# A new place in SBUF for the operands of a two-layer encoder's matrix products

## The chip, the cores and the metric

The kernel runs on one core of a Trainium2 chip. The metric is the device time of one execution in microseconds (us). The profile and the trace come from one profiled execution of the same program. Engines are named as in the profile: PE is TensorE (PEld its weight loads), DVE is VectorE, ACT is ScalarE, POOL is GpSimd, SP is SyncE, which here only issues DMAs (SPq).

## What is computed

A trunk of two layers over 512 tokens of width 1024, in float32. Each layer: RMSNorm; one input projection whose columns are shared by four token mixers (A: dense attention with 8 query and 2 key heads; B: a gated linear recurrence in both directions behind a short convolution; C: attention in a band, with sinks; D: dilated attention in three groups) and by a sigmoid gate per mixer; each mixer's output is projected to 1024, gated and summed; an output projection; the residual. Then RMSNorm and an MLP of width 4096. After the layers comes a last RMSNorm.

```python
for l in range(DEPTH):
    hn = rmsnorm(x, norm_mix_g[l])
    proj = hn @ w_in[l]
    (aq, ak, av, bx, by, cq, ck, cv, dq, dk, dv, gl) = jnp.split(proj, split_points, axis=-1)
    ya, yb, yc, yd = ...                     # the four mixers
    gates = jax.nn.sigmoid(...)              # of gl
    merged = (gates[:, :, 0] * (ya @ w_proj_a[l]) + gates[:, :, 1] * (yb @ w_proj_b[l])
              + gates[:, :, 2] * (yc @ w_proj_c[l]) + gates[:, :, 3] * (yd @ w_proj_d[l]))
    x = x + merged @ w_out[l]
    hn = rmsnorm(x, norm_mlp_g[l])
    x = x + jnp.square(jax.nn.relu(hn @ w_mlp1[l])) @ w_mlp2[l]
return rmsnorm(x, norm_final_g)
```

## The kernel before

All tokens stay in SBUF with the features on the partitions: a tile [128, 8, 512] holds 128 x 8 features of 512 tokens, 16 KiB in each partition. Every matrix product is made of split operands. A float32 number is parted into a high part, which PE's fp32r form holds, and a low part, the rest; a product is the sum of three, high weights on high input, high on low, and low on high (`mm3`, lines 175 to 183; `several`, lines 193 to 195, does the same for some groups side by side). One matmul of this kind has weights of 128x128 (the stationary operand, loaded into the array by an instruction of its own) and a moving operand of 128 x 512, and adds into one PSUM tile. A group is 8 steps of depth, 24 matmuls.

The weights come as a stream of chunks, in an order written out ahead: `raw` (a DMA on SP's queue, line 102), `whi` (a cast on ACT, line 118), `wlo` (a subtraction on DVE, line 127). Each of the three has three buffers of 4 KiB.

The moving operands are these. `xh` and `xl`, the two parts of the normed input (without its tokens' factors), stay in one place for the whole kernel; they are written by `xg_tile` (line 237) and read by the projections, by the gates and by the first half of the MLP (`m1`). `yA` to `yD` are the mixers' outputs, read by `fill`, which works through one mixer's gates and projection: for each output tile a group on x, then four steps of depth on y. `mh` and `ml` are the parts of the merged sum, read by the output projection. `h0` and `h1`, named h in the trace, are the high and low parts of a quarter of the MLP's inner layer, two buffers each, written by `m1(q)` and read by `m2(q)`; the high part enters two of the three products, the low part one. `xch` is a tile of mixer B. In the attentions, `K` is moving and `Q` stationary (lines 786 and 787), `PT` is moving and `VV` stationary (line 846). For the values V the roles are turned: x is stationary and the split weights move, 256 columns at a time.

Order of a layer: the projections and mixer B (`phase1`); attention A, woven with the fill of B; attention C with the fill of A; D with the fill of C; the end of D with the fill of D (`merge` writes that order out by hand); the output projection, at whose start the residual `xres` is loaded (eight DMAs on SP, line 1153); then the MLP, `m1` and `m2` in four quarters.

SBUF is given out by pools. A pool takes its place beside the one opened before it, upwards from the low end, or with `side="right"` downwards from the top end, and gives it back when it closes. A tile's first write waits for the last readers of the tiles that held its bytes before (`reuse_waits="tile"`). So the order in which pools are opened decides all addresses. Before, the places are, in KiB of each partition (16 KiB at the very low end are not used): constants 16 to 27, raw 27 to 39, whi and wlo 39 to 63, xh 63 to 78, xl 78 to 95, small tiles to 99; then VV to 107, yB and later yC 107 to 123, and behind them the first phase's tiles and, after these, VD, gates' tiles, yA and yD (146 to 162) and the attentions' tiles. From the top down lie mg (the sum), ml and mh (176 to 208). In the MLP, xres lies from 99 to 115, h0 from 125 to 157 and h1 from 157 to 189 (in the second layer 2 KiB higher).

Of the kernel before, what the change touches and what calls it, by code (L numbers as in the profile page):

```python
# [12 lines left out]
F32R = mybir.dt.float32r  # L13
# [4 lines left out]
PSUM = bass.MemoryType.PSUM  # L18
# [8 lines left out]

# [1 line left out]
V_GMIX, V_GMLP, V_GB, V_CW, V_CB, V_LGB, V_LAM, V_G, V_SINK = 0, 8, 16, 48, 64, 68, 84, 92, 96  # L29
NV = 104  # L30
# [1 line left out]
C_ID, C_SEL4, C_SELK, C_SEL3, C_MC, C_M1, C_M2, C_M3 = 0, 128, 132, 134, 262, 646, 902, 1030  # L32
NC_ = 1158
QKS = [("CQ", 0), ("CQ", 1)] + [(k, g) for g in range(3) for k in ("DQ", "DK")]
# attention of A and C: the stages of a step and how many steps each lags behind the first
ORD = [[(w[0], int(w[1:])) for w in o.split()] for o in (
    "v5 t3 h4 n2 e1 o6 l4 s0 q8 p7",
    "h4 v5 n2 e1 l4 q8 s0 t3 o6 p7",
)]
# steps of an attention phase, steps of its fill, steps of the fill ahead of the first one  # L40
MG = ((35, 48, 3), (41, 73, 2), (18, 47, 12))
# waits in the end of mixer D, in steps of the fill beside it, and the steps of that fill
E1, E2, E3, FN = (1, 5, 2, 15)
# products that warm the tensor engine up; parts in which the first two chunks come
WU, P0, P1 = (16, 2, 2)
# the order of the projections; pieces of mixer B after each; projections that its gates follow
P1SEQ = [("BX", 0), ("BX", 1), ("K", 0), ("K", 1), ("BX", 2), ("AQ", 0, 0), ("AQ", 0, 1), ("BX", 3), ("BY", 0),
# [28 lines left out]
class Body:  # L76
    RAWB, HLB = 3, 3

    def __init__(self, ctx, tc, w, x, vec, tab, cst, out):
        self.tc, self.nc, self.ctx = tc, tc.nc, ctx  # L80
        self.w, self.x, self.vec, self.tab, self.cst, self.out = w, x, vec, tab, cst, out
        pool = lambda n, b=1, **k: ctx.enter_context(tc.tile_pool(name=n, bufs=b, reuse_waits="tile", **k))
        self.cp = pool("cp")
        self.rawp, self.hlp = pool("rawp", self.RAWB), pool("hlp", self.HLB)
        self.xgp = pool("xgp")
        self.sm = pool("sm", 3)
        self.psp = pool("psp", 2, space=PSUM)
        self.drp = pool("drp", 2, space=DRAM)
        self.order = [(l, i) for l in range(DEPTH) for i in range(NCH)]
        self.n_load = self.n_split = self.n_lo = self.n_take = 0  # L90
        self.bq = deque()
        self.raws, self.hls = {}, {}
        self.rr = self.held = 0

# [1 line left out]
    def wload(self):  # L96
# [9 lines left out]
    def parts(self, i):  # L106
        """the first chunk is worked on in parts, for an early start"""
        n = (P0, P1, 1)[min(i, 2)]
        return [slice(p * (1024 // n), (p + 1) * (1024 // n)) for p in range(n)]
# [20 lines left out]
    def ahead(self, i):  # L130
        """the high parts of the next groups, and the loads beyond them"""
        i -= self.held
        n = len(self.order)
        while self.n_split < min(i + self.HLB, n):
            self.whi()
        while self.n_load < min(self.n_lo + self.RAWB, n):
            self.wload()
# [5 lines left out]
    def take2(self, *key):  # L143
        """two chunks that stay for several groups"""
        return [self.take(*key, u, wide=u) for u in range(2)]
# [14 lines left out]

# [1 line left out]
    def ps(self, tag, bufs=2, n=512):  # L162
# [8 lines left out]

# [1 line left out]
    def mm3(self, ps, st, mv, n, step=0):  # L173
# [10 lines left out]
    def several(self, keys, mv, cuts):  # L184
        """the groups of some chunks, side by side: each part of the depth for all of them"""
        sts = [self.wst(self.take(*key, wide=u)) for u, key in enumerate(keys)]
# [29 lines left out]

# [1 line left out]
    def smt(self, n, tag):  # L218
        return self.sm.tile([128, n], F32, tag=tag, name=tag)

    def rsqrt(self, v, n, tag):
        """v: [128, n] in SBUF, positive"""
        nv = self.nc.vector
# [10 lines left out]
    def xg_tile(self, xt, c, gcol):  # L234
        """xt [128, 512] f32: tile c of the residual; writes xg"""
        nc = self.nc
# [14 lines left out]
    def norm_cols(self):  # L251
        """1/rms of each token, as columns [128, 4]"""
        nc = self.nc
# [21 lines left out]

# [1 line left out]
    def setup(self):  # L277
# [20 lines left out]
    def derive(self):  # L298
# [6 lines left out]
        ts(out=self.d_nsink, in0=vv[:, :, V_SINK:V_SINK + 8], scalar1=-1.0, scalar2=None, op0=ALU.mult)  # L305
        # softplus(-lam) = max(-lam, 0) + log1p(exp(-|lam|)), log1p(u) = 2 atanh(u / (u + 2))
        n = DEPTH * 8
# [21 lines left out]

    # ================= projections of the mixers, and mixer B =================  # L330
    def rope(self, X1, X2, T, dst, split, perm=False):
        """X1, X2 in PSUM; T: the factors (of x1, of x2 in the first half; of x2, of x1 in the second)"""
        nc = self.nc
# [63 lines left out]
    def phase1(self, l):  # L397
# [27 lines left out]
        def head_scale(key, nh, sel, n=128):  # L425
            """1/rms of each head and token, but for the token's own factor: [128, 4 * nh]"""
            ps = self.misc()
# [19 lines left out]

        # the tokens' 1/rms, as columns, as a row, and over all partitions
        X["bx", 0], X["bx", 1] = self.several([("BX", f) for f in range(2)], self.xmv, (1, 2, 3, 4, 6))
# [9 lines left out]
        if l == 0:  # L459
            self.derive()  # L460
        # tokens in other orders: by 64 from 64 on for the first group of D, by residues for the others
        rd = self.drp.tile([S], F32, tag="rd", name="rd")
# [45 lines left out]

        # queries of C, queries and keys of D; gates of mixer B between them
        ck = p1.tile([128, S], F32, tag="T", name="ck", bufs=4)  # L510
# [17 lines left out]
    def values_ac(self):  # L528
        """values of A and C: token-major, [hi | lo]"""
        nc = self.nc  # L530
# [67 lines left out]
    def gates_b(self, f):  # L598
        """gates of a tile of mixer B; what follows goes to the queue"""
        nc, p1, l = self.nc, self.p1, self.l  # L600
# [32 lines left out]
        def s2(f, d):  # L633
            q, a, u = bs[f, d]
            # 1 - a^2 = tanh(-log a) (1 + a^2)
            nv.scalar_tensor_tensor(out=q, in0=Tg[f, d, 0], scalar=1.0, in1=q, op0=ALU.add, op1=ALU.mult)
# [61 lines left out]

    # ================= gates and projections of the branches =================
    def fill(self, l, br, y):  # L700
# [42 lines left out]

    # ================= attention =================
    def pipeline(self, steps, order):
        """steps: dicts of stages; order: (stage, its distance in steps from the first)"""
        n = len(steps)
# [6 lines left out]
    def attn_gqa(self, l, which, y):  # L754
        """8 heads, 2 key heads. A: all keys; C: a band, with sinks"""
        nc, ap = self.nc, self.ap
# [273 lines left out]
    def attn_d_end(self, y):  # L1030
        """the groups' weights: exp(m_g - M) / sum_g l_g exp(m_g - M)"""
        nc, ap = self.nc, self.ap
# [56 lines left out]
    def merge(self, a, b, na, nb, first=0):  # L1089
        """a's first step, a few of b, then na steps of a spread over nb of b; then the rest"""  # L1090
        e = 0
# [17 lines left out]

    # ================= the layer =================  # L1110
    def layer(self, l):
        nc, tc = self.nc, self.tc
        nv, ns = nc.vector, nc.scalar
        es_mix = ExitStack()
        pool = lambda es, n, b=1, **k: es.enter_context(tc.tile_pool(name=n, bufs=b, reuse_waits="tile", **k))
        self.mixp = pool(es_mix, f"mix{l}")
        self.y0p = pool(es_mix, f"y0{l}")
        with tc.tile_pool(name=f"p1{l}", bufs=1, reuse_waits="tile") as self.p1:
            self.phase1(l)
        vdp = pool(es_mix, f"vd{l}")  # L1120
        self.VD = vdp.tile([128, 13, 256], F32, tag="VD", name="VD")
# [3 lines left out]
        self.gtp = pool(es_mix, f"gt{l}")  # L1125
        y1p = pool(es_mix, f"y1{l}")
        yA = y1p.tile([128, 2, 4, S], F32R, tag="y", name="yA")
# [18 lines left out]

        es_m = ExitStack()
        xp = pool(es_m, f"x{l}")
        self.sqp = xp
# [17 lines left out]

        hp = pool(es_m, f"h{l}")
        tp = pool(es_m, f"t{l}", 2)
# [3 lines left out]
        def m1(q):  # L1173
            H[q] = [hp.tile([128, KD, S], F32R, tag=f"h{z}", name=f"h{z}", bufs=2) for z in range(2)]
            early = self.several([("M1", 0, c) for c in range(2)], self.xmv, (6,)) if q == 0 else []
# [35 lines left out]
        def last(h):  # L1211
            """the last two tiles and the final norm, by halves of the tokens"""
            N = S // 2
# [115 lines left out]

# [1 line left out]
def _pack_weights(i):  # L1331
# [136 lines left out]
```

## Time and profile before

| what | value |
|---|---|
| median of three runs | 2096.09 us (2095.13 to 2098.7) |
| span of the profiled execution, first to last instruction | 2091.4 us |
| median less that span | 4.7 us |
| PE busy | 2071.0 us (99%), 9800 matmuls |
| DVE busy | 1273.3 us (61%) |
| ACT busy | 977.9 us (47%) |
| mean granted clock of PE | 0.997 |
| DMA | 220.74 MB, 106 GB/s |

The time that goes with the runs is the span and what lies around it; the profiled execution has only its span. Matmuls are pipelined: one starts before the one ahead has ended, so that their busy times added up come to more than the span, and the distance from start to start is what counts. Clock 1.00 is full speed.

### The profile page before, as it was taken

What the parts mean: (1) busy time and instruction counts of PE and PEld (TensorE: products, weight loads), DVE (VectorE), ACT (ScalarE), POOL (GpSimd) and SP (SyncE); (2) the same over time, 40 slices, a digit from 0 to 9 for tenths busy, and PEclk for the clock granted to TensorE, in tenths of its full rate; (3) what the DMA queues carried; (4) which work ended last, traced back from release to release, by engine and by line L of the source; (5) the groups of instructions that cost most, each with busy time, mean ns of one, the idle gap of its engine ahead of it and who ended that gap; (6) DMA issues with size and microseconds to landing.
All of it is one profiled execution on the core that took longest, in us unless ns stands there. A gap on an engine that the chain in (4) does not pass through costs nothing.

```text
span 2091.4 us, 25718 instructions
## 1 busy us (share of the span) xinstructions
PE 2071.0 (99%) x9800; PEld 1711.7 (82%) x9800; DVE 1273.3 (61%) x2274; ACT 977.9 (47%) x1703; POOL 0.2 (0%) x4
## 2 busy tenths in 40 slices
PE   9999999999999999999999999999999999999997
PEld 7888889987778888888878888898877788888886
DVE  6889774575466544444658887736644665444445
ACT  4366885663534332322323667757545343322322
POOL 0000000000000000000000000000000000000000
PEclk9999999999999999999999999999999999999999
DMA  5445313122234222222325552312321432223221
GB/s 190 156 142 159 113 54 100 59 97 95 72 100 144 95 97 94 97 93 99 133 95 171 159 163 67 101 66 66 121 81 53 135 117 93 99 93 99 93 100 61
DMA packets 83407, 220.74 MB, mean 106 GB/s; under 512 B 15674, under 2 KB 17850, under 8 KB 83284
## 3 DMA queue, kind: packets, MB, share of 16 engines
q1 hardware_dynamic: 80404, 214.91, 31.6%
q10 hardware_dynamic: 2880, 4.20, 0.6%
q8 instruction: 77, 1.26, 0.3%
q14 instruction: 46, 0.38, 0.1%
HBM read 197.94 MB, written 21.12 MB: 105 GB/s over the span
## 4 chain that ended last, share of the span: by engine, by line
PE 96%; DVE 2%; ACT 1%; issue 1%; DMA 0%; SPq 0%; DVEq 0%; ACTq 0%
PE ps_mm L177 15%; PE ps_mm L179 14%; PE ps_mm L178 14%; PE ps_t L177 6%; PE ps_t L179 6%; PE ps_t L178 6%; PE ps_s L177 6%; PE ps_s L179 6%; PE ps_s L178 6%; PE ps_o L846 2%; PE ps_t L825 2%; PE ps_s L786 1%; PE ps_s L787 1%; PE ps_o L992 1%; PE ps_t L966 1%; PE ps_s L917 1%
## 5 line engine op out<-in xcount | busy, mean ns | idle before, releaser
L118 ACT CAST whi<-raw 128x1024 fp32r<-128x1024 f32 (+1 forms) x318 | 329.9, 1042 | 353.6 <-PE ps_mm L178 122.0
L127 DVE TENSOR_TENSOR wlo<-raw,whi 128x1024 fp32r<-128x1024 f32 (+1 forms) x318 | 385.0, 1214 | 106.0 <-ACT whi L118 103.3
L177 PE MATMUL ps_mm<-xh,whi 128*128 128x512 f32 x720 | 288.2, 400 | 0.0
L179 PE MATMUL ps_mm<-xh,wlo 128*128 128x512 f32 x720 | 282.0, 392 | 0.0
L178 PE MATMUL ps_mm<-xl,whi 128*128 128x512 f32 x720 | 281.8, 391 | 0.0
L177 PEld LDWEIGHTS ps_mm<-xh,whi 128*128 128x128 f32 x720 | 135.5, 188 | 32.4 <-issue 4.1
L179 PEld LDWEIGHTS ps_mm<-xh,wlo 128*128 128x128 f32 x720 | 135.6, 188 | 29.3
L178 PEld LDWEIGHTS ps_mm<-xl,whi 128*128 128x128 f32 x720 | 135.8, 189 | 26.9
L177 PE MATMUL ps_t<-xh,whi 128*128 128x512 f32 x368 | 143.7, 390 | 0.0
L178 PE MATMUL ps_t<-xl,whi 128*128 128x512 f32 x368 | 143.2, 389 | 0.0
L179 PE MATMUL ps_t<-xh,wlo 128*128 128x512 f32 x368 | 143.2, 389 | 0.0
L177 PE MATMUL ps_s<-xh,whi 128*128 128x512 f32 x352 | 138.6, 394 | 0.0
L179 PE MATMUL ps_s<-xh,wlo 128*128 128x512 f32 x352 | 137.1, 389 | 0.0
L178 PE MATMUL ps_s<-xl,whi 128*128 128x512 f32 x352 | 137.0, 389 | 0.0
L835 DVE TENSOR_TENSOR PT<-ps_t,PT 128x512 fp32r<-128x512 f32 (+2 forms) x128 | 75.2, 588 | 72.2 <-ACT PT L832 56.6
L832 ACT CAST PT<-ps_t 128x512 fp32r<-128x512 f32 (+2 forms) x128 | 63.8, 501 | 57.5 <-PE ps_o L846 56.1
L819 ACT ACTIVATE P<-P,al 128x512 f32<-128x512 f32 (+2 forms) x128 | 82.7, 646 | 12.6 <-DVE al L818 11.6
L709 DVE TENSOR_TENSOR gt<-ps_mm,rb 128x512 f32<-128x512 f32 x54 | 37.2, 688 | 80.7 <-PE ps_mm L179 80.5
L177 PEld LDWEIGHTS ps_t<-xh,whi 128*128 128x128 f32 x368 | 69.1, 188 | 17.4 <-issue 3.0
L179 PEld LDWEIGHTS ps_t<-xh,wlo 128*128 128x128 f32 x368 | 69.1, 188 | 14.4
L178 PEld LDWEIGHTS ps_t<-xl,whi 128*128 128x128 f32 x368 | 69.1, 188 | 14.3
L177 PE MATMUL ps_mm<-whi,xh 128*128 128x256 f32 (+1 forms) x224 | 79.6, 355 | 0.0
(423 smaller groups left out, 4330.7 us busy)
## 6 DMA issues: line engine op xcount, KB each, us to landing
raw<-in_w_dram SPq DMA_DIRECT2D x314, 512.0 KB, 3.5
qsA<-stk SPq DMA_DIRECT2D x32, 128.0 KB, 2.3
qsC<-stk SPq DMA_DIRECT2D x32, 128.0 KB, 2.3
K<-ks SPq DMA_DIRECT2D x16, 256.0 KB, 5.6
Q<-qsA SPq DMA_DIRECT2D x16, 256.0 KB, 4.0
Q<-qsC SPq DMA_DIRECT2D x16, 256.0 KB, 2.7
qD<-stkf SPq DMA_DIRECT2D x24, 128.0 KB, 2.2
kD<-stkf SPq DMA_DIRECT2D x24, 128.0 KB, 2.2
```

Source lines behind the costliest of these rows:

```text
L118: self.nc.scalar.copy(hi[:, s], self.raws[i][:, s])
L127: self.nc.vector.tensor_tensor(out=lo[:, s], in0=raw[:, s], in1=hi[:, s].bitcast(F32), op=ALU.subtract)
L177: mm(ps, sh, mh, start=(k == 0), stop=False)
L178: mm(ps, sh, ml, start=False, stop=False)
L179: mm(ps, sl, mh, start=False, stop=(k == n - 1))
L709: nv.tensor_tensor(out=g, in0=ps, in1=self.rb, op=ALU.mult)
L786: nc.tensor.matmul(ps[:, 0:n], qq, Kt[j][:, 0, b0 * 128:b1 * 128], start=True, stop=False)
L819: ns.activation(out=P[:, 0:n], in_=P[:, 0:n], func=AF.Copy, scale=ls)
L825: nc.tensor.transpose(pt[:, b * 128:(b + 1) * 128], P[:, b * 128:(b + 1) * 128], self.ident)
L832: ns.copy(st["dst"][0], st["src"])
L835: nv.tensor_tensor(out=st["dst"][1], in0=st["src"], in1=st["dst"][0].bitcast(F32), op=ALU.subtract)
L846: nc.tensor.matmul(o, a, b, start=(n_ == 0), stop=(n_ == len(mm) - 1))
```

## The change

Pools are opened in another order and on the other side; no instruction is added or removed, and the order on every engine and queue is the same.

In `Body.__init__` the pool of xh and xl is the first at the low end. The constants, raw, the split weights (hlp) and the small tiles (sm) go to the top end, in this order from the top down. In `layer`, the pool of yB and yC is opened ahead of the mixers' other tiles (VV and others), the pool of yA and yD right after the first phase closes, ahead of VD and the gates' tiles. In the MLP the pool of h gives way to two: `h0p` for the high parts, opened first of all, and one for the low parts, where h was.

From the sizes of the tiles the places after are, in KiB: xh 16 to 32, xl 32 to 48, yB and yC 48 to 64, VV from 64 on, the first phase from 72 on, later yA and yD 72 to 89 and VD above; in the MLP h0 48 to 80, xres 80 to 96, h1 106 to 138. From the top down: constants to 214, raw to 202, whi and wlo to 178, small tiles to 173, mg to 157, ml and mh to 125.

```diff
@@ Body.__init__
-        self.cp = pool("cp")
-        self.rawp, self.hlp = pool("rawp", self.RAWB), pool("hlp", self.HLB)
+
         self.xgp = pool("xgp")
-        self.sm = pool("sm", 3)
+        self.cp = pool("cp", side="right")
+        self.rawp, self.hlp = pool("rawp", self.RAWB, side="right"), pool("hlp", self.HLB, side="right")
+        self.sm = pool("sm", 3, side="right")
@@ layer
+        self.y0p = pool(es_mix, f"y0{l}")
         self.mixp = pool(es_mix, f"mix{l}")
-        self.y0p = pool(es_mix, f"y0{l}")
         with tc.tile_pool(name=f"p1{l}", bufs=1, reuse_waits="tile") as self.p1:
             self.phase1(l)
+        y1p = pool(es_mix, f"y1{l}")
         vdp = pool(es_mix, f"vd{l}")
...
         self.gtp = pool(es_mix, f"gt{l}")
-        y1p = pool(es_mix, f"y1{l}")
         yA = y1p.tile([128, 2, 4, S], F32R, tag="y", name="yA")
...
         es_m = ExitStack()
+        h0p = pool(es_m, f"h0{l}")
         xp = pool(es_m, f"x{l}")
...
-        hp = pool(es_m, f"h{l}")
+        hps = h0p, pool(es_m, f"h1{l}")
...
-            H[q] = [hp.tile([128, KD, S], F32R, tag=f"h{z}", name=f"h{z}", bufs=2) for z in range(2)]
+            H[q] = [hps[z].tile([128, KD, S], F32R, tag=f"h{z}", name=f"h{z}", bufs=2) for z in range(2)]
```

The rest of the diff blanks comments and keeps the line numbers.

## Rows read from the trace of the kernel before

**Rows 1.** The page: busy time by engine; the chain that ended last.

```profile
PE 2071.0 (99%) x9800; PEld 1711.7 (82%) x9800; DVE 1273.3 (61%) x2274; ACT 977.9 (47%) x1703; POOL 0.2 (0%) x4
...
PE 96%; DVE 2%; ACT 1%; issue 1%; DMA 0%; SPq 0%; DVEq 0%; ACTq 0%
```

**Rows 2.** Waits of PE over the span: who, for what, total, times, longest.

```profile
PE ps_s L786 <- DMA Q<-qsA: 5.6, 2, 3.4
```

**Rows 3.** PE's groups, shapes apart: count, busy us, mean ns of one, idle.

```profile
L178 PE MATMUL ps_mm<-xl,whi 128*128 128x512 f32 x720 | 281.8, 391 | 0.0
...
L178 PE MATMUL ps_t<-xl,whi 128*128 128x512 f32 x368 | 143.2, 389 | 0.0
...
L178 PE MATMUL ps_s<-xl,whi 128*128 128x512 f32 x352 | 137.0, 389 | 0.0
L177 PE MATMUL ps_mm<-whi,xh 128*128 128x256 f32 x192 | 70.5, 367 | 0.0
...
L179 PE MATMUL ps_mm<-h,wlo 128*128 128x512 f32 x168 | 66.7, 397 | 0.0
...
L178 PE MATMUL ps_mm<-h,whi 128*128 128x512 f32 x168 | 66.3, 395 | 0.0
...
L846 PE MATMUL ps_o<-PT,VV 128*128 128x512 f32 x128 | 32.1, 393 | 0.0
...
L178 PE MATMUL ps_mm<-yB,whi 128*128 128x512 f32 x64 | 25.3, 396 | 0.0
...
L177 PE MATMUL ps_s<-mh,whi 128*128 128x512 f32 x32 | 12.7, 397 | 0.0
```

**Rows 4.** Timeline of PE, MLP up: start, us of one; first and last.

```profile
729.62 0.39 PE L177 MATMUL ps_s<-xh,whi 128*128 128x512 f32 x1
...
741.86 0.39 PE L177 MATMUL ps_s<-xh,whi 128*128 128x512 f32 x1
```

**Rows 5.** Timeline of PE, output projection: first and last.

```profile
641.53 0.39 PE L193 MATMUL ps_s<-mh,whi 128*128 128x512 f32 x1
...
651.84 0.40 PE L195 MATMUL ps_t<-mh,wlo 128*128 128x512 f32 x1
```

**Rows 6.** Timeline of PE, MLP down: first and last.

```profile
799.69 0.40 PE L177 MATMUL ps_t<-h,whi 128*128 128x512 f32 x1
...
811.82 0.40 PE L178 MATMUL ps_s<-h,whi 128*128 128x512 f32 x1
```

**Rows 7.** Windows: length, PE, PEld, DVE, ACT, POOL busy, clock, DMA share, GB/s.

```profile
639.00:817.00 178.00, 178.00 (x773) 144.84 (x772) 97.26 (x115) 63.83 (x85) 0.00 (x0) 1.00 0.29 100
```

**Rows 8.** Timeline of PE in attention A, around a change from x to K.

```profile
212.62 0.40 PE L179 MATMUL ps_mm<-xh,wlo 128*128 128x512 f32 x1
212.85 0.39 PE L786 MATMUL ps_s<-K,Q 128*128 128x512 f32 x1
```

**Rows 9.** PE's groups within attention A, 205 to 320 us.

```profile
L178 PE MATMUL ps_mm<-xl,whi 128*128 128x512 f32 x64 | 25.1, 393 | 0.0
```

**Rows 10.** Timeline of PE in the first phase: xch between groups of x.

```profile
112.26 0.40 PE L177 MATMUL ps_mm<-xch,whi 128*128 128x512 f32 x1
...
115.06 0.40 PE L177 MATMUL ps_s<-xh,whi 128*128 128x512 f32 x1
...
116.91 0.39 PE L179 MATMUL ps_s<-xh,wlo 128*128 128x512 f32 x1
```

**Rows 11.** Timeline of SP's DMA queue at the output projection.

```profile
633.26 3.71 SPq L1153 DMA_DIRECT2D xres<-in_x_dram  x8
638.27 47.34 SPq L102 DMA_DIRECT2D raw<-in_w_dram  x9
```

**Rows 12.** Timeline of ACT at the output projection: in brackets, idle before.

```profile
652.78 1.05 ACT L118 CAST whi<-raw 128x1024 fp32r<-128x1024 f32 x1 [0.36 <-PE ps_t L194]
655.73 0.72 ACT L237 ACTIVATE xh<-xres,ve 128x512 fp32r<-128x512 f32 x1 [1.89 <-DVE xres L1163]
```

**Rows 13.** The page: DMA issues, count, KB each, median us to landing.

```profile
raw<-in_w_dram SPq DMA_DIRECT2D x314, 512.0 KB, 3.5
```

**Rows 14.** Timeline of ACT at the start of the second layer.

```profile
1050.29 1.05 ACT L118 CAST whi<-raw 128x1024 fp32r<-128x1024 f32 x1 [4.64 <-PE ps_s L194]
```

## The prediction

> **What bounds the kernel now.** I read the page first: TensorE (PE) is busy for 99% of the span, and the chain that ended last runs through it for 96% [rows 1]. The waits of PE name one that lasts: the query's load at the start of the attentions, 5.6 us in two pieces [rows 2]. So the time is the number of matmuls times the spacing from one to the next, and only what alters the spacing, or opens a gap on PE, moves the end. The page shows matmuls that overlap, so "mean ns of one" is no spacing: it holds a tail that runs beside the next. I therefore read the groups of PE by shape [rows 3], and then the timeline of stretches in which one kind follows itself, counting starts. Input x as the moving operand, MLP up: 729.62 to 741.86 us, 54 matmuls, 226.7 ns each [rows 4]. mh/ml, output projection: 641.53 to 651.84, 44 steps, 234.3 ns [rows 5]. The inner tiles h, MLP down: 799.69 to 811.82, 52 steps, 233.3 ns [rows 6]. All have 128x128 weights and 512 columns, and over 639 to 817 us, which holds all three, the granted clock is 1.00 and PE has no gap [rows 7]; so the clock, the shape or a wait can't part them. What parts them is the moving tile. The means say the same: 389 for x, 395 for h, 396 to 397 for yB and mh, 393 for PT on VV [rows 3]; a mean minus 162 is the spacing (389-227, 395-233). The whole kernel has 4512 x matmuls of this size: three products each for rows of 720, 368 and 352 [rows 3], and 192 in `several` (two groups of projections and two of the MLP a layer, eight steps of depth, three products).
>
> **Where the tiles lie.** The addresses follow from the order of the pools and the sizes of the tiles, in KiB of a partition. Before: constants 16 to 27, raw and split weights 27 to 63, x 63 to 95, and all else above 95: xch, yB, yC around 107, yA, yD 146, mh/ml 176 to 208, h 125 to 189. Weights stand low, x low beside them, everything slow is high. After: x 16 to 48, yB/yC 48 to 64, in the MLP the two high parts of h at the same 48 to 80, yA/yD 72 to 89; the low parts of h 106 to 138, mh/ml 125 to 157; and the split weights go to 178 to 202, the constants above them. The change swaps two things at once: moving tiles go low, and weights leave.
>
> **Part 1, weights to the top while x stays low.** This is the pair that sets the sum. The trace of before has no case of x against weights at the top but one: the last x matmul ahead of a K-on-Q pair, during which Q (above 170 KiB) is loaded. It starts at 212.62 us, the next at 212.85, its duration 0.40 where its neighbours have 0.39 [rows 8]: a digit, but in the direction of slower. In the attention phases, in which x alternates with PT, K, P and y, x's mean is 393 against 389 [rows 9]. On the other hand, at 112.26 us the moving tile becomes xch, high, with weights in the same place as before, and x comes back at 115.06: 12 xch matmuls take 2.80 us, 233.3 each, and x needs 8 more at 231.3 (115.06 to 116.91) before it is back at its pace [rows 10]. And PT on VV, both high, has 393, between x and the rest [rows 3]. Three readings fit: low moving tile is fast; moving tile and weights in the same part are fast; or their distance is (in steps of 512 bytes x stands at a whole multiple from the high and low weights before, every slow tile does not; PT/VV is off too). The first is contradicted by x ahead of Q, the second and third are both broken by the change for x: weights at the top, and x then 96 bytes off a multiple of 512. I take x to lose its pace and come to that of h: +6.6 ns each (233.3-226.7). From the fast side: no loss at all, 0; from the slow side: 397, the largest mean among the slow groups [rows 3], +8 ns.
>
> The sum: 1152 of the 4512 x matmuls (3 mixers x 2 layers x 64 x 3) lie in the attention phases and have half the loss already (393), so +2.6 ns to 395: +3.0 us. The other 3360 x 6.6 = +22.2 us. Together +25.2 us; ends 0 and 3360 x 8 + 1152 x 4 = +31.5.
>
> [...]
>
> **Part 2, mh/ml, y, h.** Against the weights at the top, y and the high parts of h become low tiles, as x; mh/ml, xch and the low parts of h stay high, but nearer the weights. Under the readings that I take for x, the first stay as they are (234 and 233, already slow): 0. If mh/ml get PT's pace on VV, 393 for 396: 384 matmuls (8 tiles, 8 steps, 3 products, 2 layers) x 3 ns = -1.2 us; the yA and yD come off as well or not at all. I take -1 us; ends -2 (with the 496 low parts of h by 2 ns) and 0. V's products have the weights as moving tiles, 256 columns [rows 3], 576 of them (three products of 192): at most half the loss of a 512-wide one, 3.3 ns, so 0 to +1.9 us; I take 0.5.
>
> **Part 3, waits that move.** Tiles now reuse other places, so some writes wait for other readers. The eight loads of the residual are issued on SP at 633.26 us, and the weight chunk behind them at 638.27 [rows 11]; their new place is that of VD, yD and the gates' tile, read until the last yD matmul ends about 641.7 (mh starts at 641.53 [rows 5]). So they start some 8.4 us later. Who waits: the first add, ahead of ACT's xh at 655.73, and the weight chunks queued behind them on SP, the first of which is cast at 652.78 [rows 12]. A weight chunk lands 3.5 us after its issue [rows 13], a tile of the residual, half as large, hardly later: the first residual tile is there at about 645, ten us early; the chunk, issued at 646.7 (638.27 + 8.4), at 650.2, 2.6 us early, with two chunks cast ahead of it. So 0; if the cover failed, 8.4 us a layer at worst. In the next layer the rotary tables, on ACT's queue, would wait for the store of the last residual tile, about as long as a load of its size, 2 to 3.5 us; behind the cast that follows them ACT waits 4.64 us for PE before the one at 1050.29 [rows 14]: 0. y1 opened earlier only moves addresses. Attention's tiles keep their offset to the first phase's, so the waits of Q [rows 2] stay. The order of instructions, their number and each queue's order are the same.
>
> **Sum.** +25.2 - 1 + 0.5 = +24.7 us on a span of 2091.4 us: 2116.1. The median of the runs, 2096.09, is 4.7 us above the span of the profiled execution, and I keep that distance: 2120.8, say 2121 us. Its own range: from the pace of PT on VV (+4 ns on 3360, none inside the attentions, -2 for the others: +11, 2107) to +8 ns (+31.5 and +1.9: 2129.5).
>
> **Rivals.**
> *The place of the moving tile alone decides; a low one is fast.* For it: x is the only low moving tile and the only one at 226.7 [rows 4]; every high one is slower [rows 3]. Against: x ahead of Q, and PT in between [rows 3, 8]. Then x keeps its pace and y and the high h gain: 992 h matmuls (two of three products of 1488; one of nine rows is shown) x 6.6 = -6.5 us, 768 y matmuls (four mixers, three products of 64), alternating in the attentions as x does there, x 3 to 7 = -2.3 to -5.4, weights as moving tiles +0 to 1.9. In all -4 to -11: 2085 to 2092, middle 2088. It decides when low moving tiles against high weights run under 228 ns.
> *No price.* The 6.6 ns come from something that the layout takes along, or gain and loss cancel (a loss of 2 ns per x matmul, 9 us, eats the gains of h and y). Then the time is 2096. [...]
> *The late residual uncovers.* If the loads land after the add at about 655, PE stands still at the MLP's start, up to 8.4 us in each layer, 17 in all: 2113 with x unchanged. Against: the ten us and 2.6 us of slack. This adds to the others rather than replaces them.
>
> **How the numbers follow.** Loss of x's pace 0.55, and the residual's wait 0.03: slower. Low place alone 0.30: faster. No price or cancelled 0.12. 0.2%, about 4.2 us, is what a measurement of this kernel can tell from no change; 2092 to 2100 is "same". The likeliest one's own range is 2107 to 2130. The range that leaves no more than 2 in 10 out takes in most of the low-place case: 2087 to 2130. Chances: faster 0.30, same 0.12, slower 0.58.
>
> **What would show it.** The timeline of the MLP's up stretch: x at 233 ns (mean 395), or still 226.7. The down stretch: in each triple two matmuls with h's high part; at 395 in all three rows if I am right, at 389 in two if the low place decides. mh/ml at 393. No new wait on PE beside Q's, the residual loads near 642 on SP. Wrong it is if x's mean stays at 389: then weights at the top cost nothing and only the moving tile's place, or nothing, counts.

## The result and the profile after

The changed kernel takes 2115.78 us (median of four, 2112.85 to 2116.86) against 2096.04 for the kernel before: a ratio of 1.0091, interval 1.0077 to 1.0106 (ratios and intervals here come from all runs, not from the two medians), slower by 19.7 us. The forecast was slower, 2121 us. The profiled execution has a span of 2114.3 us, 22.9 more than before's, and a time of 2116.14.

The page of the changed kernel, first lines of its parts 1 and 4 (the lines that answer to [rows 1]):

```profile
span 2114.3 us, 25718 instructions
...
PE 2095.7 (99%) x9800; PEld 1712.2 (81%) x9800; DVE 1273.9 (60%) x2274; ACT 977.9 (46%) x1703; POOL 0.2 (0%) x4
...
PE 96%; DVE 2%; ACT 1%; DMA 1%; issue 1%; SPq 0%; DVEq 0%; ACTq 0%
```

The same instructions, and PE is busy for 24.7 us more; no other engine has grown by more than 0.6. So the time went into the matmuls themselves. PE's groups by shape of the changed kernel (line numbers are one higher than before; count, busy us, mean ns, idle):

```profile
L178 PE MATMUL ps_t<-xh,whi 128*128 128x512 f32 x368 | 146.1, 397 | 0.0
L180 PE MATMUL ps_t<-xh,wlo 128*128 128x512 f32 x368 | 145.7, 396 | 0.0
L179 PE MATMUL ps_t<-xl,whi 128*128 128x512 f32 x368 | 144.8, 393 | 0.0
L178 PE MATMUL ps_mm<-whi,xh 128*128 128x256 f32 x192 | 70.3, 366 | 0.0
...
L178 PE MATMUL ps_mm<-h,whi 128*128 128x512 f32 x168 | 67.0, 399 | 0.0
...
L179 PE MATMUL ps_mm<-h,whi 128*128 128x512 f32 x168 | 66.3, 395 | 0.0
...
L180 PE MATMUL ps_mm<-h,wlo 128*128 128x512 f32 x168 | 65.7, 391 | 0.0
...
L847 PE MATMUL ps_o<-PT,VV 128*128 128x512 f32 x128 | 32.0, 392 | 0.0
...
L179 PE MATMUL ps_mm<-yB,whi 128*128 128x512 f32 x64 | 25.3, 396 | 0.0
...
L178 PE MATMUL ps_s<-mh,whi 128*128 128x512 f32 x32 | 12.6, 395 | 0.0
```

Against [rows 3]: x has gone from 389 to 393, 396 and 397 in its three products, which means 395.3; h has other values for each product and the same mean, 395; PT and yB have not moved, mh has come down by 1 to 2. The timeline of PE in the MLP's up stretch (start, us of one), which answers to [rows 4]:

```profile
735.18 0.40 PE L178 MATMUL ps_s<-xh,whi 128*128 128x512 f32 x1
735.42 0.39 PE L179 MATMUL ps_s<-xl,whi 128*128 128x512 f32 x1
735.65 0.39 PE L180 MATMUL ps_s<-xh,wlo 128*128 128x512 f32 x1
735.88 0.40 PE L178 MATMUL ps_s<-xh,whi 128*128 128x512 f32 x1
```

Three steps take 0.70 us, 233.3 ns each instead of 226.7, and they repeat: 237, 231, 232 ns by the trace's unrounded starts. Over all x matmuls whose next record follows within 300 ns, the mean goes from 227.0 to 233.4 ns outside the attentions and from 229.7 to 233.4 inside (there, between a layer's first K matmul and its last yC matmul: 1074 and 1066 pairs; outside 3315 and 3314).

The waits that the change moves, on SP's queue, on ACT at the output projection and at the start of the second layer (they answer to [rows 11, 12, 14]):

```profile
650.52 3.65 SPq L1155 DMA_DIRECT2D xres<-in_x_dram  x8
```

```profile
661.54 1.05 ACT L119 CAST whi<-raw 128x1024 fp32r<-128x1024 f32 x1 [0.35 <-PE ps_t L195]
664.48 0.72 ACT L238 ACTIVATE xh<-xres,ve 128x512 fp32r<-128x512 f32 x1 [1.89 <-DVE xres L1165]
...
1059.41 1.05 ACT L119 CAST whi<-raw 128x1024 fp32r<-128x1024 f32 x1 [2.14 <-DMA xs<-xres]
1064.15 1.05 ACT L119 CAST whi<-raw 128x1024 fp32r<-128x1024 f32 x1 [3.68 <-PE ps_s L195]
```

The residual's loads now start 0.2 us after the first mh matmul (650.33 us) instead of 8.3 us ahead of it, and no wait downstream ends with them: the third cast and the first xh wait for PE and DVE as before. In the second layer the cast behind the tables does wait 2.14 us for the store of the residual, and 3.68 us of slack behind it take that up.

### The profile page after: what moved, and what is told of

Read it like the earlier page. It is cut to its first block, busy times and chain, and to the rows that moved or that the text cites. A ratio compares the mean times of both kernels' runs of the same rounds, so it can differ in the third digit from the quotient of the medians.

```text
span 2114.3 us, 25718 instructions
## 1 busy us (share of the span) xinstructions
PE 2095.7 (99%) x9800; PEld 1712.2 (81%) x9800; DVE 1273.9 (60%) x2274; ACT 977.9 (46%) x1703; POOL 0.2 (0%) x4
## 4 chain that ended last, share of the span: by engine, by line
PE 96%; DVE 2%; ACT 1%; DMA 1%; issue 1%; SPq 0%; DVEq 0%; ACTq 0%
PE ps_mm L178 15%; PE ps_mm L180 14%; PE ps_mm L179 14%; PE ps_t L178 6%; PE ps_t L180 6%; PE ps_t L179 6%; PE ps_s L178 6%; PE ps_s L180 6%; PE ps_s L179 6%; PE ps_o L847 2%; PE ps_t L826 2%; PE ps_s L787 1%; PE ps_s L788 1%; PE ps_o L993 1%; PE ps_t L967 1%; PE ps_s L918 1%
## 5 line engine op out<-in xcount | busy, mean ns | idle before, releaser
L180 PE MATMUL ps_mm<-xh,wlo 128*128 128x512 f32 x720 | 286.3, 398 | 0.0
L178 PEld LDWEIGHTS ps_s<-xh,whi 128*128 128x128 f32 x352 | 66.1, 188 | 16.6 <-issue 1.4
```

The source lines that it names most:

```text
L178: mm(ps, sh, mh, start=(k == 0), stop=False)
L180: mm(ps, sl, mh, start=False, stop=(k == n - 1))
```

## The experiments

The readings to tell apart, from the prediction: what makes x fast is that moving tile and weights lie in the same *part* of SBUF, or their *distance*, in steps of 512 bytes. Gaps are pools with one tile that nothing uses. SBUF is full in attention A, so in all whole kernels below the softplus' small tiles get one buffer instead of three, which frees 896 bytes.

```diff
+    def gap(self, pool, nbytes):
+        t = pool.tile([128, nbytes // 4], F32, name="gap")
+        self.nc.vector.memset(t[:, 0:1], 0.0)
...
-        return self.sm.tile([128, n], F32, tag=tag, name=tag)
+        return self.sm.tile([128, n], F32, tag=tag, name=tag, bufs=1 if tag.startswith("sp") else 3)
```

**The changed kernel with distances of 512 n.**

```diff
+        self.gap(pool(f"ga", side="right"), 416)
         self.rawp, self.hlp = pool("rawp", self.RAWB, side="right"), pool("hlp", self.HLB, side="right")
         self.sm = pool("sm", 3, side="right")
+        self.gap(pool(f"gb", side="right"), 256)
...
+        self.gap(pool(es_mix, f"gc{l}"), 224)
         y1p = pool(es_mix, f"y1{l}")
...
+        if l:
+            self.gap(pool(es_m, f"gd{l}"), 288)
         hps = h0p, pool(es_m, f"h1{l}")
```

> The changed kernel with small gaps between the pools, so that every tile of x, y, mh/ml and h stands at a whole multiple of 512 bytes from the high and low weights, as x does in the kernel before. All stay in the same part of SBUF as in the changed kernel to within 1 KiB. The small tiles of the softplus get one buffer for three to make room. Theory 'distance' (the distance of moving tile and weights, in steps of 512 bytes, sets the pace): x is back at 226.7 ns and y, mh, h come to it: 2096 less 1488 x 6.6 (h), 384 x 7.6 (mh/ml) and 768 x 3 to 4 (y) ns, about 2080 us. Theory 'part' (weights and moving tile in the same part of SBUF): x stays at 233 ns, 2116 us.

Measured: 2080.07 us, ratio to the kernel before 0.9917 (0.9901 to 0.9932). Weights at the top and x at the bottom, and x is at 389 again; so are h and mh:

```profile
L185 PE MATMUL ps_t<-xl,whi 128*128 128x512 f32 x368 | 143.3, 389 | 0.0
...
L184 PE MATMUL ps_mm<-h,whi 128*128 128x512 f32 x168 | 65.4, 389 | 0.0
...
L184 PE MATMUL ps_s<-mh,whi 128*128 128x512 f32 x32 | 12.5, 389 | 0.0
```

**The kernel before with x alone moved by 96 bytes.**

```diff
+        self.gap(pool(f"ga"), 96)
         self.xgp = pool("xgp")
         self.sm = pool("sm", 3)
+        self.gap(pool(f"gb"), 288)
```

> The kernel before with x alone moved up by 96 bytes, which gives it the distance from the weights that it has in the changed kernel (96 above a multiple of 512); everything else keeps its distance from the weights. Theory 'distance': x falls to 233 ns as in the changed kernel, 2096 + 20 = 2116 us (2110 to 2120). Theory 'part': weights low and x low, nothing changes, 2096 us.

Measured: 2116.85 us, ratio 1.0098 (1.0081 to 1.0115), the time of the changed kernel. x's three products are at 394 to 397:

```profile
L185 PE MATMUL ps_t<-xh,wlo 128*128 128x512 f32 x368 | 146.2, 397 | 0.0
L183 PE MATMUL ps_t<-xh,whi 128*128 128x512 f32 x368 | 145.2, 395 | 0.0
...
L184 PE MATMUL ps_t<-xl,whi 128*128 128x512 f32 x368 | 145.1, 394 | 0.0
```

A part of SBUF can't be the reason, since x has moved by 96 bytes.

**The kernel before with y, mh/ml and h at 512 n.**

```diff
         self.sm = pool("sm", 3)
+        self.gap(pool(f"ga"), 480)
...
+        self.gap(pool(es_r, f"gb{l}", side="right"), 416)
         mgp = pool(es_r, f"mg{l}", side="right")
...
+        self.gap(pool(es_m, f"gc{l}"), (288, 64)[l])
         hp = pool(es_m, f"h{l}")
```

> The kernel before with y, mh/ml and h moved by less than 512 bytes each, to a multiple of 512 from the weights; they stay high, the weights low. Theory 'distance': h, mh/ml and y come to 226.7 ns: 1488 x 6.6 + 384 x 7.6 + 768 x 3 to 4 ns = 15 us less, 2080 us. Theory 'part': they stay at 233 to 234, 2096 us.

Measured: 2079.72 us, ratio 0.9920 (0.9906 to 0.9935). PE's groups of this kernel:

```profile
L182 PE MATMUL ps_mm<-h,whi 128*128 128x512 f32 x168 | 65.4, 389 | 0.0
L183 PE MATMUL ps_mm<-h,whi 128*128 128x512 f32 x168 | 65.4, 389 | 0.0
L184 PE MATMUL ps_mm<-h,wlo 128*128 128x512 f32 x168 | 65.4, 389 | 0.0
...
L183 PE MATMUL ps_mm<-yB,whi 128*128 128x512 f32 x64 | 25.1, 393 | 0.0
...
L182 PE MATMUL ps_s<-mh,whi 128*128 128x512 f32 x32 | 12.4, 389 | 0.0
```

h and mh, high as before, run at x's pace. The two aligned kernels agree within 0.4 us in their medians, one with the weights at the top and x, y and the high parts of h low, the other with the weights low and y, h and mh/ml high; so at this distance the place is worth nothing that these runs, which spread over 5 to 6 us each, can tell.

**A map of places and distances.** All of the kernel's work is left out; the products run on one tile of 200,000 bytes in each partition, and the core of the program is:

```python
for n, (mh, ml, wh, wl) in enumerate(CFG):
    for r in range(REPS):
        ps = self.wide()
        for k in range(KD):
            sh, sl, h, l = at(wh + 512 * k, 128), at(wl + 512 * k, 128), at(mh + 2048 * k, 512), at(ml + 2048 * k, 512)
            mm(ps, sh, h, ...); mm(ps, sh, l, ...); mm(ps, sl, h, ...)
```

> Nothing of the reference is computed and the output is zeros: groups of 24 products (whi on the high part, whi on the low part, wlo on the high part, as in the kernel) on chosen places of one filled tile, three groups for each of 62 places: distances of 0 to 496 bytes modulo 512 with both low, moving tile and weights in different parts, the two parts of the moving tile or of the weights at different distances. Theory 'distance': 226.7 ns at distance 0 wherever the tiles lie, 229 to 238 at others, the same when the weights move as when the moving tile does. Theory 'part': 226.7 for both low at any distance, 233 for low on high or high on low.

The timeline of PE in three of its cases: moving tile at 63 KiB and weights at 39 KiB, distance 96 (first and last of 49); moving tile at 63 KiB and weights at 178 KiB, distance 0 (48); the same places, distance 96 (49):

```profile
108.14 0.39 PE L1383 MATMUL ps_s<-T 128*128 128x512 f32 x1
...
119.34 0.39 PE L1383 MATMUL ps_mm<-T 128*128 128x512 f32 x1
...
410.30 0.39 PE L1384 MATMUL ps_s<-T 128*128 128x512 f32 x1
...
420.95 0.39 PE L1383 MATMUL ps_mm<-T 128*128 128x512 f32 x1
...
527.25 0.39 PE L1383 MATMUL ps_s<-T 128*128 128x512 f32 x1
...
538.45 0.39 PE L1383 MATMUL ps_mm<-T 128*128 128x512 f32 x1
```

11.20 us for 48 steps is 233.3 ns; 10.65 for 47 is 226.6; 11.20 for 48 is 233.3 again. The cases, by the starts of the last 48 of 72 matmuls:

```
distance  ns      distance  ns      places, distance 0                     ns
   0     226.7      256    226.7    moving 105, 143, 173 KiB, weights 39   226.7
  16     231.7                      moving 17, 63, 105, 143, weights 178   226.7
  32     233.4      288    233.3    places, distance 96: the same seven    233.2 to 233.3
  64     228.8      320    228.9    moving high part 0, low part 256       226.7
  96     233.2      352    233.4    moving high part 0, low part 32        233.4
 128     232.2      384    232.2    whi 0, wlo 256                         226.7
 160     234.3      416    234.3    whi 0, wlo 32                          233.4
 192     233.4      448    233.4    both moved by 96                       226.7
 224     233.3      480    233.3    weights moved by 256                   226.7
```

The pattern repeats every 256 bytes, not 512 (496 has 236.6, 240 has 236.7 in the next map). At distances of 0 and 96 it does not depend on the places, and it is the distance that counts, since moving both operands by 96 changes nothing.

**One gap in the changed kernel.** Only the first of the four gaps above, with 160 bytes.

> The changed kernel with one gap of 160 bytes between the constants and the raw weights (and one buffer for three for the softplus' small tiles, which makes the room and moves the sum and mh/ml up). x, yB, yC, the high parts of h, both parts of h in the first layer, and mh/ml then stand at a multiple of 256 bytes from the weights, yA, yD 32 above one, the low part of h in the second layer 32 below one. If a multiple of 256 is enough and the place does not count: 2116 - 20 (x back) - 768 x 6.6 (h, first layer) - 384 x 7 (mh/ml) - 384 x 3 ns (yB, yC) = 2087 us. If 512 is needed for what stands 256 off (here all of the aligned tiles do): 2116 us, no gain. Place of low tiles alone has no say left.

Measured: 2083.37 us, ratio 0.9943 (0.9927 to 0.9960). A multiple of 256 is enough: in this kernel every aligned tile stands 256 off a multiple of 512. It is 3.6 us faster than forecast: the second layer's h, whose low part alone is misplaced, has a mean of 231.1 ns for 233.3 where I had put no gain (720 matmuls, 1.6 us). For the rest, x's steps take 25.8 us less than in the changed kernel's trace, where I had put the net 20, while those of V, yD and the warm-up take 3.3 us more; what is left is within the spread of its runs (2081.88 to 2086.52).

**Finer distances, and which weights.** The same kind of program with other lists, again without the kernel's work.

> Nothing of the reference is computed and the output is zeros: groups of 24 products as before, 46 cases: distances between the steps tried so far (4 to 252 bytes), a matmul whose own weights stand at distance 0 while the weights that are loaded beside it stand at 32, 96 or 160 and the reverse, weights of 32 to 96 columns, the same weights again and again, moving operands of 128 to 480 columns. If the stream of the moving operand and the load of the next weights disturb each other: slow where the next weights stand off, 226.7 ns where the next stand at 0 whatever the own do; narrow weights lose the dependence. If it is the own weights: the reverse. If the cost belongs to the pair of products and not to the load: no difference with the weights' columns.

```
distance  ns     distance  ns     case                                     ns
   4     238.0      72    235.5   own weights 0, next weights 32, 96, 160  231.6, 234.0, 234.1
   8     232.7      80    231.2   own weights 32, 96, 160, next weights 0  230.0, 230.1, 229.9
  12     228.9     112    231.2   same weights all along, 0 and 96         226.7, 233.3
  20     240.0     144    233.3   32 columns of weights, 0 and 96          231.6, 233.3
  24     234.2     176    233.3   64 columns of weights, 0 and 96          230.0, 230.0
  28     228.6     208    234.7   256 columns moving, 0 and 96             120.0, 119.9
  40     232.3     244    240.0   384 columns moving, 0 and 96             173.3, 176.6
  56     231.6     252    230.5   480 columns moving, 0 and 96             216.6, 220.0
```

None of the 29 other residues tried in the two maps comes nearer to 226.7 than 228.6, and the worst cost 13 ns. Of the two expectations on own and next weights neither holds alone: the next weights, those loaded beside the stream (in the kernel before, at 735.06 us, a weight load of 0.19 us starts with the matmul ahead of its own), cost more when they stand off (231.6 to 234.1), but their standing right does not give 226.7 back (230). With 64 columns of weights the dependence on the distance is gone, and so is the fast pace; with 32 and with 96 (230.0 and 231.2 ns) a part of it, 1.7 and 1.2 ns, is left. So narrower weights don't simply lose it, as one expectation had it. With 256 columns or fewer moving there is none (128 columns: 111.6 and 111.6).

**x off by 64 bytes.** The second experiment with 64 and 320 for 96 and 288. **All operands aligned.** The third with multiples of 256, and gaps of 64 ahead of VV, 128 ahead of xch, 192 ahead of the constants, and the rests to a multiple of 256 behind them.

> The kernel before with x alone moved up by 64 bytes; everything else keeps its distance from the weights. In the map of places a distance of 64 bytes gave 228.8 ns for 226.7 at 0 and 233.2 at 96. If the map carries over to the kernel as a price list: 3360 x 2.2 ns and about 1 us in the attentions, 2096 + 8 = 2104 us. If any distance off a multiple costs the same: 2116 us as with 96 bytes. If the small step counts for nothing: 2096 us.

> The kernel before with everything that PE streams in products of 256 columns or more at a multiple of 256 bytes from its weights: what was aligned in the kernel of before with small gaps (y, mh/ml, h, K on Q), and now also PT on VV, mixer B's xch, and the constants against P. Order and places otherwise as before. If the distance is all: the earlier one's 2080 us less 192 x 3 ns (PT on VV) and 96 x 6 ns (xch), 1 to 2 us more from x, y and K between them: 2077 to 2079 us. If what is left inside the attentions (x at 229.4 ns there) comes from the change of kinds and not from distances: 2079 to 2080 us.

Measured: 2104.90 us for x off by 64, ratio 1.0034 (1.0021 to 1.0048), 7.6 us above the kernel before: the map's price for 64 bytes carries over (x at 229.3 ns outside the attentions, for 228.8 in the map). All aligned: 2079.01 us, ratio 0.9916 (0.9903 to 0.9928), not told apart from the third experiment's 2079.72. PT on VV is at 390 for 392 there, and x inside the attentions stays at 229.5. What is left there comes from the change of kinds, that is, from the matmuls of other operands and shapes in between: in this kernel's trace the first two x steps behind such a change take 232.2 and 232.6 ns, and from the tenth on they take 227.0.

The map is a price list only to about 1 ns. At 128 bytes (modulo 256) it has 232.2 to 232.4, also at the very places of before's h in the first layer and of the changed kernel's mh/ml; in their kernels these two run at 233.3. In the two kernels with x moved, where that h lies 512 bytes lower and so at the same distance, it runs at 232.4. Each pace holds for all groups of its kernel; what decides between the two is not shown.

## Why the prediction was right, and where its sizes were off

**x loses its pace: shown.** +6.4 ns measured outside the attentions for +6.6 forecast, and +3.7 for +2.6 inside: 3360 x 6.4 + 1152 x 3.7 = 25.8 us against 25.2. The span grew by less, 22.9: PE's wait for Q is 0.7 us shorter, the steps of V, mh/ml and xch 0.4 us each, and smaller differences go the same way, a spell of 1.6 us at a granted clock of 0.50 the other. The change costs this through 96 bytes, not through the move: the second experiment has the change's loss (20.75 us over its kernel before) with x 96 bytes from its old place and nothing else at another distance from the weights.

**Of the three readings only the distance stands.** The prediction left "same part" and "distance" open, since both gave the same sum, and put the distance in steps of 512 bytes, where 256 is enough. Part is refuted by the second experiment, the map and the two aligned kernels. Its best row for the part, x ahead of Q [rows 8], was a row of the distance: Q stood at 96 bytes from x. The trace's four x steps ahead of K on Q with 512 columns take 235.2 ns before and 226.8 in the third experiment, where Q is aligned too. PT on VV at 64 had 393, and mh at 416 had a spacing of 234.3, the map's 234.3 [rows 3, 5]. But x's 393 in the attentions [rows 9], read as half of the loss, was not: it stays when all is aligned (395, 394 and 390 in that stretch of the all-aligned kernel), and comes from the change of kinds. The size, "x comes to the pace of h", was luck in part: 96 bytes happens to cost what h at 128 and 352 cost; at 64 bytes it would have been about a third.

**mh/ml, y, h, V: small, as forecast.** mh/ml came down to 395 rather than 393; h's three products share the same sum; V's products, 366 for 367, lost nothing where I had put 0.5. The 768 y matmuls of the prediction (and of two expectations) count D's like the others; the trace has 672, since D's y is two steps deep, not four, and at 3 to 7 ns that is 0.3 to 0.7 us.

**The waits: shown hidden.** The residual's loads went where the prediction put them, behind the last yD matmul, and the 2 us at the tables appear on ACT (2.14 us) with slack behind them (3.68 us). A residual tile landed a median 5.3 us after its issue before and 4.8 us after the change, for the 3.5 of the estimate; the first add (663.77 us) starts 13 us after the first load (650.52). PE's wait for Q is 4.9 us, for 5.6 [rows 2].

**The step that was mis-sized is the last one, from span to time.** I kept 4.7 us between the median and the span. For every execution of a whole kernel here the time is 1.7 to 1.9 us above its own span (2116.14 and 2114.3; 2080.86 and 2079.1); before's profiled execution was simply one of its quick ones, by 2.9 us. Of the 5.2 us between 2121 and 2115.8, 2.9 are that; most of the rest is that the span came to 2114.3 for 2116.1 forecast.

**The rivals.** A low place alone: the changed kernel refutes it, and the aligned kernels show no price of the place; its own terms add up to -7 to -12 us, not the -4 to -11 of the prediction. No price: the second experiment refutes it, 96 bytes alone cost 20.75 us. The residual's wait: not there.

What stays open is why. The runs show a price per matmul that depends on the distance of two addresses modulo 256 bytes, on the own and the next weights, and on the width of both operands; they don't show what in the chip makes it.

## What to carry to other kernels

Where PE sets the end and matmuls of this kind (128x128 weights, loaded for each, and 384 moving columns or more; at 256 there was no difference, 120.0 and 119.9 ns) follow one another, give all moving tiles and all weights the same address modulo 256 bytes of a partition; here that took 16 to 18 us off the kernel (0.8%) with its work unchanged. A change of layout that looks like one of order or place changes these residues too, so take the spacing from start to start per tile before and after, and tell the residue from the place by moving one tile by a few dozen bytes. And take the distance from span to time from the same execution, not from the median of others.

## What the runs showed of the hardware that was not expected

Spacings of one shape go from 226.7 to 240.0 ns with nothing changed but the distance of two operands (0 and 20 bytes); the mean granted clock of the two maps is 0.998 and 0.995. A distance of 4 bytes costs more (238.0) than one of 64 (228.8).

Spells at a granted clock of 0.50 come and go. The mean granted clock differs between executions of one kernel (0.996 to 0.998 in the changed kernel's four), and the changed kernel's profile has a spell in attention A that the profile of before has not; timeline of PE and windows of that stretch (the clock is the third figure from the end):

```profile
213.00 0.47 PE L787 MATMUL ps_s<-K,Q 128*128 128x512 f32 x1 [2.76 <-DMA Q<-qsA]
...
214.66 0.63 PE L179 MATMUL ps_mm<-xl,whi 128*128 128x512 f32 x1
215.09 0.63 PE L180 MATMUL ps_mm<-xh,wlo 128*128 128x512 f32 x1
```

```profile
214.25:217.65 3.40, 3.40 (x10) 2.66 (x8) 3.37 (x7) 3.37 (x5) 0.00 (x0) 0.50 0.97 249
...
218.00:230.00 12.00, 12.00 (x60) 9.77 (x59) 7.62 (x19) 9.69 (x20) 0.00 (x0) 1.00 0.44 148
```

After a wait of 2.76 us for Q and five matmuls, eight matmuls run at a granted clock of 0.50, 427 ns apart, which costs some 1.6 us; before had the same wait in the same place, 2.2 us long in this layer and 3.4 in the second [rows 2], without a spell. The profiles of the whole kernels have none to three of them ahead of the end (one in before's, at 1074.85 us, and two in the changed kernel's). They may be part of the spread of a few us between executions; no run separates that.
